# A hybrid decoder trunk on one core: the scan's outputs moved next to the transposes of the next pair of chunks

## The chip, the cores and the metric

The kernel runs on one core of a Trainium2 chip. The metric is the device time of one execution in microseconds (us); several executions are timed and their median is given.

## The reference, cut to what is computed

One sequence of 2048 tokens, width 1024, passes two layers, each `x + RMSNorm_post(mixer(RMSNorm_pre(x)))`. The second mixer is sliding-window attention; the change does not touch it. The first is a Mamba-2 state-space mixer with 32 heads in 8 groups, 16 chunks of 128 tokens:

```python
cb = einsum('bclgn,bcsgn->bcgls', Cc, Bc)                               # scores of a chunk
y_diag = einsum('bcgrls,bcsgrp->bclgrp', cb[:, :, :, None] * decay, x)
states = einsum('bclgn,bcgrl,bclgrp->bcgrpn', Bc, decay_to_end, x)
def step(h, inp):
    s, d = inp
    return h * d[..., None, None] + s, h                                # the scan over chunks
y_off = einsum('bclgn,bcgrpn,bcgrl->bclgrp', Cc, h_in, exp(a_cs))
y = y_diag + y_off
```

Before the scan stand the input projection, a causal convolution of 4 taps and SiLU; after it a gate, a norm and the output projection.

## The kernel before

The first layer takes the tokens in two halves (`hf`) of 1024, and in each the 8 groups one after the other. For a group, `ssm_proj` multiplies the normed input with six blocks of 128 weight columns (B, C, x0, x1, z0, z1), each for two blocks of 512 tokens. All of it is in float32 split into a high and a low part, so a block of 512 tokens is 24 products of 128x512 (three for each of eight row blocks, `mm3`, lines 88 to 92). A block's weights come by a DMA (`wraw`, two buffers), ScalarE makes the high part (`whi`, L150) and GpSimd the low one (`wlo`, L152). The results are evicted by ScalarE (`raw`, `sx`, or the gate `zz`, L733), convolved by VectorE (L749, L753).

`ssm_scan` runs one group behind: while group g is projected, the scan of group g-1 is fed in. It is a generator, and `interleave` calls its next step whenever the projection has advanced by another share of its cost; `SCAN` is the number of steps that the scan of one group has. The steps are:

- `load(c)`: a DMA on SyncE's queue brings `ab` (the cumulative decays of chunk c in 128 partitions). There are four buffers; chunk c+4 takes that of chunk c, which the outputs of chunk c read last.
- `stage1(c)`: on TensorE three transposes and the scores into one PSUM tile `pt` (L779, L780, L783, L784); from it VectorE makes `xd`, `bl`, `xw`, `cbm`, `xl` and ScalarE `bh` (L793) and `xh` (L801). `xl` is the last of this chain (`xw`, then `xh`, then `xl`). From `ab` ScalarE makes the decays: four Relu (L809, the only readers that wait for the load), an Exp on `ab` (L814) and one on `dec` (L816); GpSimd multiplies `ab` (L815), VectorE `dec` (L817).
- `states(c)`: six products `sps` for chunks c and c+1 from `xh`, `xl`, `bh`, `bl`.
- `state(c)`: VectorE adds (`hn`), GpSimd decays (`hd`).
- `outputs(c)`: sixteen small products of 64 output columns, `yt` (L856, L861), for the pair c, c+1; VectorE (L868) and GpSimd (L870) finish `ysb`, and a DMA stores it.

For each pair of chunks four steps come in this order: states and the first state; the second state with stage1 of chunk c+2; stage1 of chunk c+3; outputs of the pair with the loads of c+4 and c+5. Inside `tc.high_priority(offset=60)` stage1's other engines get precedence. The order on each engine is then set by a scheduler, and each engine and the DMA queue keep that order.

The change touches `ssm_scan` (its main loop) and the constant `SCAN`; `run` uses it for each group, and `SCAN - 7` for the rest of the last group's scan, which is fed into the first output pieces (`u`, L251).

Of the kernel before, what the change touches and what calls it, by code (L numbers as in the profile page):

```python
# [35 lines left out]
QW = 1024  # L36
KVW = 256
AIN = 2560
SCAN = 19

# [6 lines left out]
def interleave(main, cost, side, n_side):  # L49

    done, at = 0, 0.0
    for w in main:
        at += w
        want = min(n_side, int(at * n_side / cost))
        while done < want:
            next(side, None)
            done += 1
    drain(side)


class Trunk:
# [694 lines left out]
    def ssm_scan(self, sp, yp, tabs, hf, g, res, yT):  # L756
# [6 lines left out]
        def load(c):  # L763
            if c < 8:
                ab = sp.tile([P, 4, P], F32, tag="ab", name="ab", bufs=4)
                j = c * 8 + g
                nc.sync.dma_start(ab.rearrange("p r l -> p (r l)"), atd[j].partition_broadcast(P))
                abs_.append(ab)

        def stage1(c):  # L770
            if c > 7:
                return
            ab = abs_[c]
            s, o = divmod(c, 4)
            sl = slice(o * P, (o + 1) * P)
            x0, x1, Bt, Ct = (res[n, s] for n in ("x0", "x1", "B", "C"))
            pt = (yp.tile([P, 4, P], F32, tag="y", name="pt", bufs=2) if c % 2
                  else self.tp.tile([P, 4, P], F32, tag="tr", name="pt"))
            nc.tensor.transpose(pt[:, 0, :], x0[:, sl], self.ident)  # L779
            nc.tensor.transpose(pt[:, 1, :], x1[:, sl], self.ident)  # L780
            last = hf == 1 and c == 7
            if not last:
                nc.tensor.transpose(pt[:, 2, :], Bt[:, sl], self.ident)  # L783
            nc.tensor.matmul(pt[:, 3, :], Bt[:, sl], Ct[:, sl], start=True, stop=True)  # L784
            with self.tc.high_priority(offset=60):
                xv = pt[:, 0:2, :].rearrange("p a (h d) -> p (a h) d", d=64)
                xd = sp.tile([P, 4, 64], F32, tag="xd", name="xd", bufs=4)
                hb = dt[:, c, 4 * g:4 * g + 4].unsqueeze(2).to_broadcast([P, 4, 64])
                nc.vector.tensor_tensor(xd, xv, hb, ALU.mult)
                bx = None  # L790
                if not last:
                    bh = sp.tile([P, P], F32R, tag="bh", name="bh")
                    nc.scalar.activation(bh, pt[:, 2, :], AF.Copy)  # L793
                    bl = sp.tile([P, P], F32R, tag="bl", name="bl")
                    nc.vector.tensor_tensor(bl, pt[:, 2, :], bh.bitcast(F32), ALU.subtract)
                    xw = sp.tile([P, 4, 64], F32, tag="xw", name="xw", bufs=1)
                    hb = w2[:, c, 4 * g:4 * g + 4].unsqueeze(2).to_broadcast([P, 4, 64])
                    nc.vector.tensor_tensor(xw, xv, hb, ALU.mult)
                    xf = xw.rearrange("p h d -> p (h d)")
                    xh = sp.tile([P, 256], F32R, tag="xh", name="xh")  # L800
                    nc.scalar.activation(xh, xf, AF.Copy)  # L801
                    xl = sp.tile([P, 256], F32R, tag="xl", name="xl")
                    nc.vector.tensor_tensor(xl, xf, xh.bitcast(F32), ALU.subtract)
                    bx = bh, bl, xh, xl
                cbm = sp.tile([P, P], F32, tag="cbm", name="cbm", bufs=1)
                nc.vector.tensor_tensor(cbm, pt[:, 3, :], self.triu, ALU.mult)
                dec = sp.tile([P, 4, P], F32, tag="dec", name="dec", bufs=4)
                for r in range(4):
                    nc.scalar.activation(dec[:, r, :], ab[:, r, :], AF.Relu, scale=-1.0,  # L809
                                         bias=acs[:, c, 4 * g + r:4 * g + r + 1])  # L810
                ce = None
                if not (hf == 0 and c == 0):
                    ce = ab
                    nc.scalar.activation(ce, ab, AF.Exp)  # L814
                    nc.gpsimd.tensor_tensor(ce, ce, Ct[:, sl].unsqueeze(1).to_broadcast([P, 4, P]), ALU.mult)  # L815
                nc.scalar.activation(dec, dec, AF.Exp, scale=-1.0)  # L816
                nc.vector.tensor_tensor(dec, dec, cbm.unsqueeze(1).to_broadcast([P, 4, P]), ALU.mult)  # L817
            sts.append((xd, bx, dec, ce))

        def states(c):  # L820

            sps = yp.tile([P, 2, 256], F32, tag="st", name="sps")
            for u in range(2):
                if sts[c + u][1]:
                    self.mm3(sps[:, u, :], *sts[c + u][1], True, True)
            return sps

        def decayed(c, h):
            if h is None or c > 7 or (hf == 1 and c == 7):
                return None  # L830
            hd = sp.tile([P, 4, 64], F32, tag="hd", name="hd", bufs=1)
            hb = cd[:, c, 4 * g:4 * g + 4].unsqueeze(2).to_broadcast([P, 4, 64])
            nc.gpsimd.tensor_tensor(hd, h.rearrange("p (h d) -> p h d", d=64), hb, ALU.mult)
            return hd

        def state(c, add, hd):

            if hf == 1 and c == 7:
                return None, None
            hn = self.hsave[g] if (hf == 0 and c == 7) else sp.tile([P, 256], F32, tag="hst", name="hn", bufs=3)  # L840
            if hd is None:
                nc.vector.tensor_copy(hn, add)
            else:
                nc.vector.tensor_tensor(hn, hd.rearrange("p h d -> p (h d)"), add, ALU.add)
            return hn, decayed(c + 1, hn)

        def outputs(c0, hps):

            yt = yp.tile([P, 2, 2 * P], F32, tag="y", name="yt", bufs=2)
            for u in range(2):  # L850
                xd, _, dec, ce = sts[c0 + u]
                for pr in range(2):
                    yo = yt[:, pr, u * P:(u + 1) * P]
                    for e in range(2):
                        r = 2 * pr + e
                        nc.tensor.matmul(yo[64 * e:64 * e + 64], xd[:, r, :], dec[:, r, :],  # L856
                                         start=True, stop=ce is None)
                    if ce is not None:
                        for e in range(2):
                            r = 2 * pr + e  # L860
                            nc.tensor.matmul(yo[64 * e:64 * e + 64], hps[u][:, 64 * r:64 * r + 64], ce[:, r, :],  # L861
                                             start=False, stop=True)
            s, o = divmod(c0, 4)
            sl = slice(o * P, (o + 2) * P)
            ysb = sp.tile([P, 2, 2 * P], F32, tag="ysb", name="ysb")
            for pr in range(2):
                yv = ysb[:, pr, :]
                nc.vector.scalar_tensor_tensor(yv, res[f"x{pr}", s][:, sl], self.dch[:, 2 * g + pr:2 * g + pr + 1],  # L868
                                               yt[:, pr, :], ALU.mult, ALU.add)
                nc.gpsimd.tensor_tensor(yv, yv, res[f"z{pr}", s][:, sl], ALU.mult)  # L870
            t0 = (8 * hf + c0) * P
            nc.sync.dma_start(
                yT[2 * g * P:(2 * g + 2) * P, t0:t0 + 2 * P].rearrange("(a p) t -> p a t", p=P), ysb)
# [1 line left out]
        for c in range(4):  # L875
            load(c)
        stage1(0)
        yield
        stage1(1)
        yield  # L880
        hprev = self.hsave[g] if hf else None
# [2 lines left out]
        for c in range(0, 8, 2):  # L884
            sps = states(c)
            h0 = hprev
            h1, hd = state(c, sps[:, 0, :], hd)
            yield
            hprev, hd = state(c + 1, sps[:, 1, :], hd)
            stage1(c + 2)  # L890
            yield
            stage1(c + 3)
            yield
            outputs(c, (h0, h1))
            load(c + 4)
            load(c + 5)
            yield


# [8 lines left out]
    def run(self, ctx):  # L908
# [19 lines left out]
        with ExitStack() as actx:  # L928
# [35 lines left out]
            for hf in range(2):  # L964
                tabs = {}
                hs, hnext = hnext, []
                for g in range(NG):
# [10 lines left out]
                    cost = 56 if g == 0 else 52 if hf and g == NG - 1 else 58  # L978
                    interleave(self.ssm_proj(ap, hs, hf, g, res, preps, dtg, tail, start), cost, side, SCAN)
                    if dtg:  # L980
# [7 lines left out]
            def head():  # L988
# [5 lines left out]
                yield from pieces[1]  # L994
            interleave(head(), 15, side, SCAN - 7)
        wn = self.bcast(cp, io["pre_norm"][1], tag="wn")
# [62 lines left out]
```

## Time and profile before

| | |
|---|---|
| median of 3 runs | 2584.83 us (2583.25 to 2587.38) |
| the profiled execution | 2584.72 us |
| its span, first to last instruction | 2583.0 us |
| mean granted TensorE clock | 0.995 of full speed |
| the states' products (first and last start) | 117.6 to 1402.2 us of the span |

The page's first part gives each engine's busy time, its fourth the chain of work that ended last. The other views are a timeline of instructions, the instructions of one tile with what they waited for, and busy time by stretches.

### The profile page before, as it was taken

How to read it: one execution, taken by the hardware profiler on the slowest of the kernel's cores; microseconds unless marked ns; L12 is line 12 of the kernel's file. 1: busy time of each engine (PE TensorE's matmuls, PEld its weight loads, DVE VectorE, ACT ScalarE, POOL GpSimd, SP SyncE). 2: the span in 40 equal slices, each digit the busy share in tenths (PEclk: the TensorE clock that was granted, in tenths of full speed). 3: DMA queues.
4: the chain of work that ended last, by engine and by line, in shares of the span. 5: the costliest groups of instructions: out<-in, count | busy, mean ns of one | idle time of the engine just before them, and what ended most of it. 6: DMA issues, size and time to landing. Idle time of an engine off the chain costs nothing.

```text
span 2583.0 us, 38760 instructions
## 1 busy us (share of the span) xinstructions
PE 2527.8 (98%) x14083; PEld 2107.9 (82%) x14083; DVE 1673.7 (65%) x3363; ACT 1274.9 (49%) x3195; POOL 921.6 (36%) x817
## 2 busy tenths in 40 slices
PE   7999999999999999999999999999999999999998
PEld 6878888888777888888887888888888888888787
DVE  6677666766776667666678544447777777767422
ACT  5455555555645555555566422324554455545321
POOL 2344444444434454444445222222222112220222
PEclk9999999999999999999999999999999999999999
DMA  4332223223423222222325332234111121111343
GB/s 127 96 86 64 81 76 87 74 70 78 116 62 105 78 83 77 78 78 78 82 78 174 113 101 90 90 128 140 54 54 58 54 78 54 54 32 58 123 146 120
DMA packets 266656, 224.46 MB, mean 87 GB/s; under 512 B 31136, under 2 KB 229984, under 8 KB 266464
## 3 DMA queue, kind: packets, MB, share of 16 engines
q1 hardware_dynamic: 266464, 221.98, 29.2%
q8 instruction: 111, 1.82, 0.3%
q14 instruction: 81, 0.66, 0.1%
HBM read 179.72 MB, written 42.21 MB: 86 GB/s over the span
## 4 chain that ended last, share of the span: by engine, by line
PE 74%; DVE 10%; POOL 5%; DMA 4%; ACT 4%; issue 4%; SPq 0%; POOLq 0%; ACTq 0%; DVEq 0%
PE u L251 19%; PE ps L90 14%; PE ps L92 14%; PE ps L91 14%; DVE sx L749 2%; DMA ab<-atd 2%; POOL wlo L152 2%; PE sc L420 2%; PE yt L856 2%; PE yt L861 1%; PE ot L474 1%; PE ot L478 1%; DVE dec L817 1%; PE tt L453 1%; POOL ab L815 1%
## 5 line engine op out<-in xcount | busy, mean ns | idle before, releaser
L90 PE MATMUL ps<-hi,whi 128*128 128x512 f32 (+1 forms) x1808 | 725.5, 401 | 9.4 <-ACT whi L150 4.7
L92 PE MATMUL ps<-hi,wlo 128*128 128x512 f32 (+1 forms) x1808 | 706.1, 391 | 4.2 <-POOL wlo L152 4.2
L91 PE MATMUL ps<-lo,whi 128*128 128x512 f32 (+1 forms) x1808 | 704.6, 390 | 0.2 <-DVE lo L140 0.2
L92 PEld LDWEIGHTS ps<-hi,wlo 128*128 128x128 f32 x1808 | 340.7, 188 | 80.2 <-POOL wlo L152 6.1
L90 PEld LDWEIGHTS ps<-hi,whi 128*128 128x128 f32 x1808 | 341.2, 189 | 77.9 <-issue 15.9
L152 POOL TENSOR_TENSOR wlo<-wraw,whi 128x1024 fp32r<-128x1024 f32 x114 | 282.6, 2479 | 319.1 <-ACT whi L150 310.6
L749 DVE SCALAR_TENSOR_TENSOR sx<-raw,cw,sx 128x512 f32<-128x512 f32 x384 | 342.9, 894 | 71.3 <-ACT sx L746 66.5
L91 PEld LDWEIGHTS ps<-lo,whi 128*128 128x128 f32 x1808 | 341.6, 189 | 55.2 <-DVE lo L140 0.8
L251 PE MATMUL u<-ol,yh 128*128 128x512 f32 x768 | 239.6, 393 | 1.0 <-DVE ol L223 0.9
L251 PE MATMUL u<-oh,yh 128*128 128x512 f32 x768 | 240.5, 394 | 0.0
L251 PE MATMUL u<-oh,yl 128*128 128x512 f32 x768 | 237.6, 391 | 0.0
L809 ACT ACTIVATE dec<-ab,acs 128x128 f32<-128x128 f32 x512 | 165.4, 392 | 128.9 <-DMA ab<-atd 114.3
L815 POOL TENSOR_TENSOR ab<-ab,sx 128x512 f32<-128x512 f32 x120 | 168.9, 1409 | 154.5 <-ACT ab L814 140.5
L752 ACT ACTIVATE raw<-sx 128x512 f32<-128x512 f32 x128 | 80.6, 630 | 221.4 <-DVE sx L749 221.3
L90 PE MATMUL ps<-qh,hi 128*128 128x384 f32 x512 | 181.1, 355 | 0.0
L870 POOL TENSOR_TENSOR ysb<-ysb,zz 128x256 f32<-128x256 f32 x128 | 108.1, 861 | 197.9 <-DVE ysb L868 197.7
L235 POOL TENSOR_TENSOR yl<-yr,yh 128x1024 fp32r<-128x1024 f32 (+1 forms) x64 | 119.3, 1864 | 161.3 <-ACT yh L233 161.2
L233 ACT ACTIVATE yh<-yr 128x1024 fp32r<-128x1024 f32 (+1 forms) x64 | 54.1, 845 | 242.3 <-PE u L251 189.3
L91 PE MATMUL ps<-ql,hi 128*128 128x384 f32 x512 | 172.1, 337 | 0.9 <-POOL ql L332 0.9
L251 PEld LDWEIGHTS u<-ol,yh 128*128 128x128 f32 x768 | 143.9, 188 | 34.3 <-DVE ol L223 2.6
L92 PE MATMUL ps<-qh,lo 128*128 128x384 f32 x512 | 171.9, 336 | 0.0
L251 PEld LDWEIGHTS u<-oh,yl 128*128 128x128 f32 x768 | 144.5, 188 | 31.4
(213 smaller groups left out, 4527.7 us busy)
## 6 DMA issues: line engine op xcount, KB each, us to landing
wraw<-in_ssm_w_in SPq DMA_DIRECT2D x98, 512.0 KB, 4.1
ab<-atd SPq DMA_DIRECT2D x128, 256.0 KB, 4.6
xt<-in_x SPq DMA_DIRECT2D x32, 512.0 KB, 4.8
yT<-ysb SPq DMA_DIRECT2D x64, 256.0 KB, 2.5
yr<-yT SPq DMA_DIRECT2D x32, 512.0 KB, 4.0
xt<-x SPq DMA_DIRECT2D x32, 512.0 KB, 4.0
oraw<-in_ssm_w_out SPq DMA_DIRECT2D x16, 512.0 KB, 5.9
x<-xt SPq DMA_DIRECT2D x32, 256.0 KB, 2.1
```

The lines of the kernel that those rows point to most:

```text
L90: nc.tensor.matmul(ps, sh, mh, start=first, stop=False)
L91: nc.tensor.matmul(ps, sh, ml, start=False, stop=False)
L92: nc.tensor.matmul(ps, sl, mh, start=False, stop=last)
L152: nc.gpsimd.tensor_tensor(lo, raw, hi.bitcast(F32), ALU.subtract)
L233: nc.scalar.activation(yh, yr, AF.Copy)
L235: nc.gpsimd.tensor_tensor(yl, yr, yh.bitcast(F32), ALU.subtract)
L251: nc.tensor.matmul(st["u"][h], y[:, k, :], w[:, j, 512 * h:512 * h + 512], start=k0 + k == 0 and m == 0, stop=k0 + k == kt - 1 and m == 2)
L749: nc.vector.scalar_tensor_tensor(sx, raw[:, j:j + BLK], self.cw[:, j, ct:ct + 1], sx, ALU.mult, ALU.add)
L752: nc.scalar.activation(th, sx, AF.Tanh)
L809: nc.scalar.activation(dec[:, r, :], ab[:, r, :], AF.Relu, scale=-1.0, bias=acs[:, c, 4 * g + r:4 * g + r + 1])
L815: nc.gpsimd.tensor_tensor(ce, ce, Ct[:, sl].unsqueeze(1).to_broadcast([P, 4, P]), ALU.mult)
L870: nc.gpsimd.tensor_tensor(yv, yv, res[f"z{pr}", s][:, sl], ALU.mult)
```

## The change

stage1 of chunks 0 and 1 now share one step; in the loop the second state is a step by itself; then one step holds the outputs of the pair, stage1 of the next two chunks and the loads; then a step is empty. The states of the next pair follow. Nothing is computed otherwise.

```diff
--- before.py
+++ after.py
@@ -36,7 +36,7 @@
 QW = 1024
 KVW = 256
 AIN = 2560
-SCAN = 19
+SCAN = 18
 
 
 
@@ -875,7 +875,6 @@
         for c in range(4):
             load(c)
         stage1(0)
-        yield
         stage1(1)
         yield
         hprev = self.hsave[g] if hf else None
@@ -887,13 +886,14 @@
             h1, hd = state(c, sps[:, 0, :], hd)
             yield
             hprev, hd = state(c + 1, sps[:, 1, :], hd)
+            yield
+
+            outputs(c, (h0, h1))
             stage1(c + 2)
-            yield
             stage1(c + 3)
-            yield
-            outputs(c, (h0, h1))
             load(c + 4)
             load(c + 5)
+            yield
             yield
 
 
```

What this makes of the order on the engines is shown at three places for one and the same group, the fourth of the first half. The number behind a tile's name tells its buffers apart.

TensorE, at the outputs of one pair (`yt`), before: the last outputs and what follows them.

```order
L856 MATMUL yt_4141<-dec_4007,xd_3993 64x128 x2
L861 MATMUL yt_4141<-ab_3871,hn_4080 64x128 x2
L856 MATMUL yt_4141<-dec_4007,xd_3993 64x128 x2
L861 MATMUL yt_4141<-ab_3871,hn_4080 64x128 x2
L90 MATMUL ps_4134<-hi_262,whi_4102 128x512
L91 MATMUL ps_4134<-lo_263,whi_4102 128x512
```

And now, at the outputs of chunks 4 and 5:

```order
L856 MATMUL yt_3960<-dec_3824,xd_3810 64x128 x2
L861 MATMUL yt_3960<-ab_3647,hn_3892 64x128 x2
L779 MATMUL pt_3983<-ident_83,sx_3028 128x128
L780 MATMUL pt_3983<-ident_83,sx_3121 128x128
L783 MATMUL pt_3983<-ident_83,sx_2691 128x128
L784 MATMUL pt_3983<-sx_2852,sx_2691 128x128
L779 MATMUL pt_4011<-ident_83,sx_3028 128x128
L780 MATMUL pt_4011<-ident_83,sx_3121 128x128
L783 MATMUL pt_4011<-ident_83,sx_2691 128x128
L784 MATMUL pt_4011<-sx_2852,sx_2691 128x128
L90 MATMUL ps_3953<-hi_108,whi_3949 128x512
```

The outputs were followed by projection products; now the two stage1 of chunks 6 and 7 (`pt_3983`, `pt_4011`) follow them directly. Thirty projection products stand between these and the states' first product.

ScalarE, from `bh` of chunk 6 to the next group's decays, before (`bh_3937`, `xh_3943` are of chunk 6, `bh_3995`, `xh_4001` of chunk 7, `ab_4210`, `ab_4212` the next group's chunks 0 and 1):

```order
L793 ACTIVATE bh_3937<-pt_3930 128x128
L150 ACTIVATE whi_4102<-wraw_4100 128x1024
L742 ACTIVATE raw_3964<-ps_3896 128x512
L801 ACTIVATE xh_3943<-xw_3941 128x256
L744 ACTIVATE halo_345<-ps_3896 128x3
L746 ACTIVATE sx_3968<-ps_3896,cb_333,cw_332 128x512
L793 ACTIVATE bh_3995<-pt_3988 128x128
L801 ACTIVATE xh_4001<-xw_3999 128x256
L733 ACTIVATE zz_4057<-ps_3981 128x512
L752 ACTIVATE raw_3964<-sx_3968 128x512
L809 ACTIVATE dec_4237<-ab_4210,acs_888 128x128 x4
L809 ACTIVATE dec_4287<-ab_4212,acs_888 128x128
```

And now (`xh_3996` is of chunk 6, `xh_4024` of chunk 7):

```order
L793 ACTIVATE bh_3990<-pt_3983 128x128
L793 ACTIVATE bh_4018<-pt_4011 128x128
L809 ACTIVATE dec_4237<-ab_4210,acs_888 128x128 x3
L801 ACTIVATE xh_3996<-xw_3994 128x256
L809 ACTIVATE dec_4237<-ab_4210,acs_888 128x128
L809 ACTIVATE dec_4263<-ab_4212,acs_888 128x128
L816 ACTIVATE dec_4237<-dec_4237 128x512
L809 ACTIVATE dec_4263<-ab_4212,acs_888 128x128 x2
L733 ACTIVATE zz_4057<-ps_3953 128x512
L801 ACTIVATE xh_4024<-xw_4022 128x256
```

Both `xh` stood ahead of every instruction on the next group's `ab`. Now three Relu on `ab_4210` stand ahead of chunk 6's `xh`, and three more, an Exp, two further Relu and a gate `zz` ahead of chunk 7's.

SyncE's queue, the loads of those `ab`, before:

```order
L872 DMA yT_57<-ysb_3863 128x2x256
L148 DMA wraw_4325<-in_ssm_w_in 128x8x128
L767 DMA ab_4210<-atd0_59 128x512
L767 DMA ab_4212<-atd0_59 128x512
L872 DMA yT_57<-ysb_4051 128x2x256
```

And now:

```order
L872 DMA yT_57<-ysb_3771 128x2x256
L148 DMA wraw_4185<-in_ssm_w_in 128x8x128
L148 DMA wraw_4336<-in_ssm_w_in 128x8x128
L767 DMA ab_4210<-atd0_59 128x512
L767 DMA ab_4212<-atd0_59 128x512
L767 DMA ab_4214<-atd0_59 128x512
L872 DMA yT_57<-ysb_3977 128x2x256
```

`ab_4210` stood behind the store of a pair and one weight load, and now behind a store and two. A weight load waits for the `wlo` that last read its buffer.

## Rows read from the trace of the kernel before

**Rows 1.** The page, part 1: busy us, share of the span and instructions of each engine

```profile
PE 2527.8 (98%) x14083; PEld 2107.9 (82%) x14083; DVE 1673.7 (65%) x3363; ACT 1274.9 (49%) x3195; POOL 921.6 (36%) x817
```

**Rows 2.** The page, part 4: who holds the chain that ended last

```profile
PE 74%; DVE 10%; POOL 5%; DMA 4%; ACT 4%; issue 4%; SPq 0%; POOLq 0%; ACTq 0%; DVEq 0%
```

**Rows 3.** Timeline, PE, projection products: start us, us, engine, line, operation, tile

```profile
603.10 0.39 PE L90 MATMUL ps<-hi,whi 128*128 128x512 f32 x1
603.32 0.39 PE L91 MATMUL ps<-lo,whi 128*128 128x512 f32 x1
```

**Rows 4.** Tile sps on PE, 0 to 1360 us: idle before it, until what

```profile
  DVE xl L803: 2.6, 7
  ACT xh L801: 1.8, 3
```

**Rows 5.** The same from 1360 to 1420 us (the scan's last group)

```profile
  DVE xl L803: 2.2, 2
  DVE hn L844: 2.0, 1
```

**Rows 6.** Waits: who waited, for whom, us in total, times, longest

```profile
ACT dec L809 <- DMA ab<-atd: 114.3, 55, 7.9
```

**Rows 7.** Tile ab: its transfers from issue to landing

```profile
DMA to landing us min/median/max: 3.0/4.6/8.6
```

**Rows 8.** Timeline, a load of ab and the ScalarE instruction that waits for it

```profile
646.93 1.01 SPq L767 DMA_DIRECT2D ab<-atd  x2
...
652.03 1.28 ACT L809 ACTIVATE dec<-ab,acs 128x128 f32<-128x128 f32 x4 [3.50 <-DMA ab<-atd]
```

**Rows 9.** Timeline, chunks 6 and 7 of one group: POOL, PE and SP

```profile
579.60 2.38 POOL L152 TENSOR_TENSOR wlo<-wraw,whi 128x1024 fp32r<-128x1024 f32 x1 [0.70 <-ACT whi L150]
...
581.67 0.39 PE L861 MATMUL yt<-ab,hn 128*64 128x128 f32 x4
...
582.01 0.38 SPq L148 DMA_DIRECT2D wraw<-in_ssm_w_in  x1
...
582.45 0.57 SPq L767 DMA_DIRECT2D ab<-atd  x1
```

**Rows 10.** Timeline, ACT, the same group

```profile
584.42 0.42 ACT L801 ACTIVATE xh<-xw 128x256 fp32r<-128x256 f32 x1 [0.92 <-DVE xw L798]
...
587.48 1.56 ACT L809 ACTIVATE dec<-ab,acs 128x128 f32<-128x128 f32 x5
588.95 0.62 ACT L816 ACTIVATE dec<-dec 128x512 f32<-128x512 f32 x1
589.47 0.97 ACT L809 ACTIVATE dec<-ab,acs 128x128 f32<-128x128 f32 x3
...
592.53 0.58 ACT L733 ACTIVATE zz<-ps 128x512 f32<-128x512 f32 x1
```

**Rows 11.** Timeline, DVE, the low half xl of chunk 7

```profile
585.17 0.41 DVE L803 TENSOR_TENSOR xl<-xw,xh 128x256 fp32r<-128x256 f32 x1
```

**Rows 12.** Timeline, PE, the two projection products after outputs

```profile
629.55 0.50 PE L90 MATMUL ps<-hi,whi 128*128 128x512 f32 x1
629.89 0.40 PE L91 MATMUL ps<-lo,whi 128*128 128x512 f32 x1
```

**Rows 13.** Timeline, PE, attention: 64-column products, then transposes of 128 columns

```profile
2037.67 0.60 PE L478 MATMUL ot<-pp,vt 128*64 128x256 f32 x4
2038.21 0.98 PE L136 MATMUL pt<-ident,xt 128*128 128x128 f32 x7
```

**Rows 14.** Timeline, a VectorE instruction beside a GpSimd one

```profile
627.78 2.73 POOL L152 TENSOR_TENSOR wlo<-wraw,whi 128x1024 fp32r<-128x1024 f32 x1 [6.08 <-ACT whi L150]
...
628.19 2.60 DVE L803 TENSOR_TENSOR xl<-xw,xh 128x256 fp32r<-128x256 f32 x1
```

**Rows 15.** Timeline, PE, the projection's wait after the scan of group 0, second half

```profile
818.97 0.50 PE L90 MATMUL ps<-hi,whi 128*128 128x512 f32 x1 [2.66 <-ACT whi L150]
```

**Rows 16.** Windows: length, busy us of PE, PEld, DVE, ACT, POOL, granted clock, DMA share

```profile
821.00:826.00 5.00, 4.55 (x36) 3.57 (x36) 5.00 (x8) 3.21 (x6) 2.78 (x2) 0.66 0.40 105
```

More of the change, by code (lines that the diff above doesn't have):

```diff
@@ L889, in ssm_scan @@
             hprev, hd = state(c + 1, sps[:, 1, :], hd)
-            stage1(c + 2)
-            yield
-            stage1(c + 3)
             yield
             outputs(c, (h0, h1))
+            stage1(c + 2)
+            stage1(c + 3)
             load(c + 4)
             load(c + 5)
+            yield
             yield
```

## The prediction

> **What bounds the kernel now.** I read the page first. TensorE is busy 98% of the span, the next engine 65% [rows 1], and it holds 74% of the chain that ended last [rows 2]. So the kernel is TensorE's stream of products with some holes, and a microsecond in which TensorE stands still is a microsecond of the result. Work on the other engines counts only where TensorE waits for it.
>
> The timeline of TensorE gives the price of the stream: projection products start 0.22 to 0.23 us apart [rows 3]; I use 0.227. Then I looked for the holes that the scan makes, in the tile `sps`, the states' products: up to 1360 us they waited 2.6 us for `xl` and 1.8 us for `xh` [rows 4], in the last group, where few projection products are left as cover, 2.2 us for `xl` and 2.0 us for `hn` [rows 5]. That is all the scan's own chains cost TensorE today, about 9 us, or 0.35%. A change of order can win no more than this and a few turnarounds; it can lose more.
>
> Last, the waits: ScalarE stood 114 us, in 55 waits, for the load of `ab` [rows 6]. Today this costs TensorE nearly nothing, since `xh`, on which the states hang, is ahead of those Relu in ScalarE's order.
>
> **The change part by part.** The number of products, evictions and DMAs stays. What moves is order, and with it the time between a result and its use.
>
> *Turnaround after the outputs.* The outputs use 64 columns of the array. The projection product behind them is followed by the next only 0.34 us later [rows 12] instead of 0.227: 0.11 lost. In attention such products are followed by transposes, as here from now on: seven take 0.98 us [rows 13], the last one's own 0.27 among them: six spacings in 0.71, 0.118 each against 0.109 undisturbed, so some 0.055 is lost. 48 of the 64 outputs have a next pair: 48 x 0.055 = **2.6 us won**.
>
> *The time left for `xl`.* Both stage1 of a pair now stand at one place, and thirty projection products ahead of the states. Counted from the end of the outputs: the transposes and scores are ten passes of about 0.11 (1.0, or 0.9 after the overlap with the outputs' tail), thirty products 6.8, four state products ahead of the one that needs the second chunk's `xl` about 0.12 each. So this `xl` must be there at **8.2 us**. Before, the second stage1 had the same thirty products or these and an output group, but its VectorE and ScalarE work was that of one chunk; now two chunks and the eviction of the outputs share the stretch. For the chunks 0 and 1 nothing waits for a load there, and I count nothing.
>
> *Chunks 6 and 7, first half.* ScalarE now has three Relu on the next group's first `ab` ahead of chunk 6's `xh`, and three more, an Exp, two Relu and a gate ahead of chunk 7's. That `ab` is loaded into the buffer that the outputs directly ahead release, behind a weight load that waits for `wlo`. In the present order `wlo` ended at 581.98, the outputs at 582.06, the weight load was issued at 582.01 and `ab` at 582.45 [rows 9]. I take the same: issue 0.4 after the outputs. The Relu of such a load began 5.1 us after its issue (646.93 to 652.03) [rows 8]; the median to landing is 4.6 [rows 7]. So the first Relu starts at 5.5. Five Relu take 1.5, an Exp leaves ScalarE after 0.52, a gate takes 0.55, `xh` 0.42 [rows 10]: three Relu to 6.4, `xh` to 6.75, two Relu to 7.35, the Exp to 7.9, two Relu to 8.5, the gate to 9.05, `xh` of chunk 7 to 9.45, its `xl` 0.41 [rows 11] to 9.85. Against 8.2 TensorE stands 1.65 us. This happens in the groups 0 to 6 of the first half (for group 7 no table is ready; in the second half chunk 7 makes no state): 7 x 1.65 = **11.6 us lost**. Bounds: if `ab` lands after 3.0 us, the least seen [rows 7], the wait is gone (0); if `wlo` is 0.7 us later, since it now follows a longer burst, 2.35 each, 16.
>
> *Chunks 2 and 3.* ScalarE has an `ab` ahead of the two `xh` here too: chunk 5's, released with the outputs' end in the first half, chunk 4's, released half an output group (0.9) earlier in the second. First half: Relu at 5.15, `xh` of 2 to 5.8, three Relu 6.7, two Exp 7.75, `xh` of 3 to 8.2, `xl` 8.6: 0.4 late. Second half, by the same rows, 8.5: 0.3. Over 15 groups **5 us lost**; bounds 0 and 12. For chunks 4 and 5 the same count ends at 8.2; nothing.
>
> The upper bound there comes from VectorE beside GpSimd: an `xl` of 0.41 took 2.60 us and ended with the `wlo` that had begun just before it [rows 14]. In the new order the multiplication of `ab` on GpSimd falls onto chunk 3's `xl`. I take none of this into the sum, as the bursts may miss each other. The Trainium skill (SBUF — State Buffer, Who interferes with whom) says that a VectorE instruction with two SBUF inputs and a GpSimd instruction that reads SBUF hold a shared port one after the other, the later one blocked to the end of the earlier; the row agrees, and by the rule alone each of these `xl` would end about 0.4 us later, an estimate of 6 us more.
>
> *The last group.* Its outputs, states and transposes stand with few other products between. Chunk 2 and 3's states come 14 short-step products (3.2 us) after the transposes, while four Relu on an `ab` loaded after the outputs stand ahead of `xh`: by the count above 1.7 us for the first chunk and 2 for the second. With the present waits in the two other pairs I take **4 us lost**; bounds -2 and 8.
>
> *What goes away.* The present waits of `sps` before the last group, **4.4 us won** [rows 4]; they sat at chunks whose `xl` now waits for something else.
>
> *The weights after group 0* of each half: the projection waited 2.66 us for `whi` and about as long for `wlo` [rows 15]. `whi` now has one `bh` and `xh` less ahead of it, but `wlo` has two `ysb` multiplications ahead of it on GpSimd. I count 0, between -4 and +3.
>
> Sum: 11.6 + 5 + 4 - 4.4 - 2.6 = +13.6 us. The profiled execution took 2584.72, practically the median of the runs (2584.83); so **2598.5 us**, 0.5% slower.
>
> **The rivals.** A change of 0.2% (5 us) is about what a measurement of this kernel can tell from none.
>
> *No change.* The loads land in time. The wait at chunks 6 and 7 is zero if `ab` is there 3.85 us after the outputs, 3.4 after its issue. For it: the least landing time is 3.0. Against it: the median is 4.6, and 55 waits today [rows 6] show that ScalarE's order reaches for these loads too early. Then +5 at most from chunks 2 and 3 stands against 7 won: 2580 to 2590. The Trainium skill (DMA: Bandwidth & Descriptors, Latency and other measured facts) puts a transfer's fixed cost at about 2 us; an `ab` near that would make this rival true, but the rows of this load say 3.0 to 8.6.
>
> *Faster.* Loads are now asked for four steps ahead of their chunk's stage1 instead of two, so ScalarE is freer at the places where `whi` was late [rows 15], and the pairs' bursts fall where projection covers them. All of the `sps` waits, the turnaround and 4 us at the weights: -11, 2574. It decides whether `xh` of chunk 7 is done before 7.8 us after the outputs.
>
> *Slower still.* The holes at chunks 6 and 7 halve the clock. After the wait of 2.66 us, with another behind it, the granted clock over 5 us was 0.66 of full speed [rows 16], so part of it was at 1.2 GHz; some 1.6 us was lost by that. Seven times 1.6, and GpSimd's blocks of 6 us: +31, 2615.
>
> **How the numbers follow.** The forecast, 2591 to 2610: 0.45. Slower still: 0.15. No change: 0.20. Faster: 0.20. Range 2577 to 2620: it leaves out most of the faster case's end and the far end of the slowest. Faster by over 0.2%: 0.2; within: 0.2; slower: 0.6.
>
> **What would show it.** In the new profile `sps` waits on TensorE for `xh` and `xl` with 15 us or more, at one place per group of the first half, some 9 us after the outputs; ScalarE's wait for `ab` ends just ahead of an `xh`. The product after the transposes starts without the 0.11. Wrong it would be if the holes at `sps` are below 5 us in all, or if `ab` lands within 3.5 us of the outputs.

## The result, and the profile after

The changed kernel takes 2668.72 us (median of 4 runs, 2665.64 to 2671.05) against 2584.34 in runs of the kernel before on the same chip: 1.0326 of it, 95% interval 1.0313 to 1.0338. The prediction was 2598.5 and at most 2620: the sign was right, the loss is six times the one forecast, and it lies above the dearest rival, 2615.

First the page of the changed kernel, part 1, which answers to [rows 1]: busy us, share of the span (2669.1 us, 86.1 more than before) and instructions of each engine.

```profile
PE 2561.5 (96%) x14083; PEld 2131.5 (80%) x14083; DVE 1711.9 (64%) x3363; ACT 1270.9 (48%) x3195; POOL 929.0 (35%) x817
```

TensorE's instructions are 14083 as before, but they are busy 33.7 us longer, and TensorE stands 52.4 us longer (107.6 idle against 55.2). So there are two losses: holes, and products that take longer. The mean granted clock fell from 0.995 to 0.982. Part 4 of the page answers to [rows 2]: TensorE held 74% of the chain and now holds 65%.

```profile
PE 65%; DVE 12%; POOL 7%; ACT 6%; DMA 5%; issue 5%; SPq 0%; POOLq 0%; ACTq 0%; DVEq 0%
```

The tile `sps` on PE, whole span (idle us before it, times), answers to [rows 4, 5], and the view of the waits (us in total, times, longest) to [rows 6]:

```profile
  ACT xh L801: 45.4, 24
  DVE xl L803: 5.8, 5
  DVE hn L844: 1.8, 1
```

```profile
ACT dec L809 <- DMA ab<-atd: 58.7, 39, 5.1
```

The states' products waited 9.2 us in the whole span of the kernel before and wait 53.0 now, nearly all for `xh`: 43.8 of the 52.4. ScalarE waits for `ab` *less* than before (58.7 against 114.3): what counts is not how long it waits but what stands behind. By the starts of the states (how much longer than undisturbed a pair's states take from the product ahead of them to their last one), chunks 6 and 7 of the first half and chunk 6 of the second hold nearly all the holes, one place in a group, as forecast for the first half and not for the second.

By stretches of the timeline (us; each boundary is the first state product of chunks 2 and 3 of the group named, the last one the first product `u`; the rest runs to the end of the span):

| | to group 1 | five groups, to group 6 | to group 1, second half | four groups, to group 5 | to `u` | rest |
|---|---|---|---|---|---|---|
| before | 224.4 | 408.0 | 277.5 | 324.8 | 141.2 | 1207.1 |
| after | 229.9 | 437.8 | 300.5 | 340.6 | 151.3 | 1208.9 |

Below, **M** is the second column, five like groups in which nothing else happens: 29.8 us lost there, 6 per group.

Now one such place, chunks 6 and 7 of group 3, in the timeline of the changed kernel; it answers to [rows 8 to 11]. The lines are sorted by engine. Columns: start us, us, engine, line, operation, tile, in brackets the idle time before it and what ended it.

```profile
430.52 0.39 PE L861 MATMUL yt<-ab,hn 128*64 128x128 f32 x4
430.84 0.33 PE L779 MATMUL pt<-ident,sx 128*128 128x128 f32 x1
431.01 0.27 PE L780 MATMUL pt<-ident,sx 128*128 128x128 f32 x1
...
431.92 0.47 PE L90 MATMUL ps<-hi,whi 128*128 128x512 f32 x1
432.23 0.39 PE L91 MATMUL ps<-lo,whi 128*128 128x512 f32 x1
...
438.62 0.39 PE L92 MATMUL ps<-hi,wlo 128*128 128x512 f32 x1
441.52 0.39 PE L90 MATMUL sps<-xh,bh 128*128 128x256 f32 x1 [2.52 <-ACT xh L801]
...
444.00 0.58 PE L90 MATMUL sps<-xh,bh 128*128 128x256 f32 x1 [1.51 <-ACT xh L801]
...
445.06 0.63 PE L90 MATMUL ps<-hi,whi 128*128 128x512 f32 x1
445.48 0.63 PE L91 MATMUL ps<-lo,whi 128*128 128x512 f32 x1
...
432.06 2.40 POOL L152 TENSOR_TENSOR wlo<-wraw,whi 128x1024 fp32r<-128x1024 f32 x1 [2.24 <-ACT whi L150]
...
434.48 0.37 SPq L148 DMA_DIRECT2D wraw<-in_ssm_w_in  x1
434.95 7.16 SPq L767 DMA_DIRECT2D ab<-atd  x3
...
437.48 0.42 ACT L793 ACTIVATE bh<-pt 128x128 fp32r<-128x128 f32 x2
440.18 0.98 ACT L809 ACTIVATE dec<-ab,acs 128x128 f32<-128x128 f32 x3 [2.28 <-DMA ab<-atd]
441.07 0.40 ACT L801 ACTIVATE xh<-xw 128x256 fp32r<-128x256 f32 x1
...
443.54 0.40 ACT L801 ACTIVATE xh<-xw 128x256 fp32r<-128x256 f32 x1
...
433.22 2.57 DVE L749 SCALAR_TENSOR_TENSOR sx<-raw,cw,sx 128x512 f32<-128x512 f32 x2 [1.34 <-ACT sx L746]
435.71 0.48 DVE L868 SCALAR_TENSOR_TENSOR ysb<-sx,dch,yt 128x256 f32<-128x256 f32 x1
436.10 0.75 DVE L749 SCALAR_TENSOR_TENSOR sx<-raw,cw,sx 128x512 f32<-128x512 f32 x1
436.76 0.75 DVE L789 TENSOR_TENSOR xd<-pt,dt 128x256 f32<-128x256 f32 x2
...
438.42 0.42 DVE L798 TENSOR_TENSOR xw<-pt,w 128x256 f32<-128x256 f32 x1
```

The outputs end at 430.91. The weight load that stands ahead of `ab` on SyncE's queue waits for the `wlo` of 432.06 to 434.46, so `ab` is issued at 434.95, 4.0 us after the outputs. The three Relu begin 5.2 later, at 440.18, chunk 6's `xh` at 441.07: 10.2 us after the outputs. The states were due at 438.85. Chunk 7's `xh` comes 2.5 us later, behind the other Relu, the Exp and the gate. But VectorE is late as well: it had the convolution and an eviction of the outputs ahead and began chunk 6's `xw` only at 438.42. Two of its convolution instructions took 2.57 together, with the `wlo` of 432.06 beside them, where the next took 0.75 alone: about 1.1 us of the lateness. Over the kernel the mean of these instructions rose from 894 to 1025 ns. And after the holes the products start 0.42 apart instead of 0.227: the lower of the two clock levels, 1.2 instead of 2.4 GHz. The window behind them (length, busy us of PE, PEld, DVE, ACT, POOL, granted clock, DMA):

```profile
446.00:452.00 6.00, 6.00 (x19) 4.71 (x18) 0.81 (x2) 1.55 (x2) 1.65 (x3) 0.66 0.00 0
```

### The profile page after: what moved, and what is told of

Its sections match the earlier page's. It is cut to its first block, busy times and chain, and to the rows that moved or that the text cites. A ratio compares the mean times of both kernels' runs of the same rounds, so it can differ in the third digit from the quotient of the medians.

```text
span 2669.1 us, 38619 instructions
## 1 busy us (share of the span) xinstructions
PE 2561.5 (96%) x14083; PEld 2131.5 (80%) x14083; DVE 1711.9 (64%) x3363; ACT 1270.9 (48%) x3195; POOL 929.0 (35%) x817
## 4 chain that ended last, share of the span: by engine, by line
PE 65%; DVE 12%; POOL 7%; ACT 6%; DMA 5%; issue 5%; SPq 0%; POOLq 0%; ACTq 0%; DVEq 0%
PE u L251 19%; PE ps L90 11%; PE ps L91 11%; PE ps L92 11%; DVE sx L749 4%; DMA ab<-atd 4%; POOL wlo L152 3%; PE sc L420 2%; ACT dec L809 1%; PE yt L856 1%; POOL hd L833 1%; PE ot L474 1%; PE yt L861 1%; POOL ab L815 1%; PE ot L478 1%
## 5 line engine op out<-in xcount | busy, mean ns | idle before, releaser
L92 PE MATMUL ps<-hi,wlo 128*128 128x512 f32 (+1 forms) x1808 | 714.9, 395 | 8.6 <-POOL wlo L152 8.6
L91 PE MATMUL ps<-lo,whi 128*128 128x512 f32 (+1 forms) x1808 | 714.5, 395 | 0.2 <-DVE lo L140 0.2
L749 DVE SCALAR_TENSOR_TENSOR sx<-raw,cw,sx 128x512 f32<-128x512 f32 x384 | 393.3, 1025 | 54.6 <-ACT sx L746 48.2
L92 PEld LDWEIGHTS ps<-hi,wlo 128*128 128x128 f32 x1808 | 346.9, 192 | 87.7 <-POOL wlo L152 13.4
L90 PEld LDWEIGHTS ps<-hi,whi 128*128 128x128 f32 x1808 | 348.8, 193 | 74.3 <-issue 8.2
L91 PEld LDWEIGHTS ps<-lo,whi 128*128 128x128 f32 x1808 | 348.0, 192 | 60.2 <-DVE lo L140 0.8
L809 ACT ACTIVATE dec<-ab,acs 128x128 f32<-128x128 f32 x512 | 176.2, 394 | 83.5 <-DMA ab<-atd 58.7
```

The costliest lines, as they stand in the source:

```text
L90: nc.tensor.matmul(ps, sh, mh, start=first, stop=False)
L91: nc.tensor.matmul(ps, sh, ml, start=False, stop=False)
L92: nc.tensor.matmul(ps, sl, mh, start=False, stop=last)
L749: nc.vector.scalar_tensor_tensor(sx, raw[:, j:j + BLK], self.cw[:, j, ct:ct + 1], sx, ALU.mult, ALU.add)
```

## The experiments

Theory A: `xh` of chunks 6 and 7 stands behind Relu that wait for the next group's `ab`. Theory B: the work of two chunks in one stretch is what is late. Theory C, formed after the first four runs: the chain over VectorE from the transposes to `xl` does not fit into 30 products, whatever waits. Beside them, the clock. Ratios are to the kernel before, 95% interval in brackets; `sps` is the idle time before the states.

| run | median us | ratio | `sps` us | clock | M us |
|---|---|---|---|---|---|
| before | | 1 | 9.2 | 0.995 | 408.0 |
| after | 2668.7 | 1.0326 [1.0313, 1.0338] | 53.0 | 0.982 | 437.8 |
| e1 `xh` first everywhere | 2648.6 | 1.0260 [1.0245, 1.0275] | 34.3 | 0.988 | 426.3 |
| e2 six `ab` | 2658.5 | 1.0301 [1.0286, 1.0316] | 55.1 | 0.989 | 427.8 |
| e3 stage1 split | 2675.5 | 1.0362 [1.0347, 1.0378] | 62.9 | 0.985 | 440.2 |
| e4 weights on GpSimd's queue | 2641.1 | 1.0232 [1.0215, 1.0249] | 34.6 | 0.990 | 427.7 |
| e5 three steps | 2610.0 | 1.0110 [1.0095, 1.0125] | 4.9 | 0.993 | 407.5 |
| e6 stage1 first | 2613.3 | 1.0124 [1.0109, 1.0139] | 18.0 | 0.990 | 404.1 |
| e7 e1 and e3 | 2675.9 | 1.0365 [1.0348, 1.0383] | 59.0 | 0.984 | 432.8 |
| e8 filled holes | 2644.5 | 1.0246 [1.0231, 1.0261] | 19.3 | 0.994 | 426.7 |
| e9 stage1 first at 6, 7 | 2603.1 | 1.0081 [1.0066, 1.0097] | 15.0 | 0.992 | 403.4 |
| e10 merge only | 2601.6 | 1.0080 [1.0066, 1.0093] | 19.8 | 0.992 | 405.4 |
| e11 e6 in first half | 2587.5 | 1.0025 [1.0015, 1.0036] | 7.8 | 0.995 | 404.1 |
| e12 e5 in first half | 2591.2 | 1.0034 [1.0022, 1.0047] | 5.0 | 0.994 | 407.5 |
| e13 Relu held for chunks 0, 1 | 2635.5 | 1.0195 [1.0179, 1.0210] | 29.2 | 0.989 | 421.8 |
| e14 merge undone | 2664.0 | 1.0309 [1.0295, 1.0324] | 57.9 | 0.989 | 434.4 |
| e15 e9 and e14 | 2638.6 | 1.0213 [1.0199, 1.0227] | 46.6 | 0.990 | 416.0 |
| e16 best by stage | 2579.9 | 0.9982 [0.9974, 0.9991] | 6.0 | 0.994 | 405.4 |

**e1.** A tiny copy makes each chunk's Relu wait for an earlier `xl`.

```diff
+ self.xls.append(xl)
...
+ k = -2 if hf == 1 and c in (0, 7) else -3
+ held = self.xls[k:k + 1]
+ if held:
+     nc.vector.tensor_copy(dec[0:1, :, 0:1], held[0][0:1, 0:4].bitcast(F32).unsqueeze(2))
  for r in range(4):
...
+ self.xls = []
```

> The changed kernel, with one VectorE copy of four numbers from the xl of two chunks before into dec ahead of the Relu, so that no Relu on a chunk's ab can stand ahead of the xh of the chunk two before. Theory A (xh of chunks 6 and 7 stands behind Relu that wait for the next group's ab): the holes at sps, 53 us in the changed kernel, fall below 15 us, time at half clock from 98 us to below 40 us, 2575 to 2595 us. Theory B (two chunks' stage1 and the eviction in one stretch make VectorE late, whatever ScalarE's order): holes above 30 us remain, now ended by xl, and the time stays above 2640 us.

A miss for theory A: 20 us back, not 75. For theory B the size came (34.3 us, above 2640), but more of the holes end at `xh` (18.5) than at `xl` (14.2). Nor is the test clean: the 126 copies take 41 us of VectorE. At chunk 6 the groups 0 to 6 of the first half have no hole left, but the order of everything moved, and chunks 4 and 5 now lose some 1.1 and 1.3 us in each group, by starts. Timeline there:

```profile
415.15 0.38 PE L91 MATMUL sps<-xl,bh 128*128 128x256 f32 x1 [0.92 <-DVE xl L803]
...
412.53 2.56 DVE L803 TENSOR_TENSOR xl<-xw,xh 128x256 fp32r<-128x256 f32 x1
...
412.28 2.53 POOL L152 TENSOR_TENSOR wlo<-wraw,whi 128x1024 fp32r<-128x1024 f32 x1 [0.88 <-ACT whi L150]
```

An `xl` of 0.41 [rows 11] took 2.56 and ended 0.28 us after the `wlo` beside it, as in [rows 14]. The Trainium skill (SBUF — State Buffer, Who interferes with whom) has this as one port pair held by one of the two; the rows agree, 2.15 us for one instruction.

**e2.** Loads one pair earlier.

```diff
- ab = sp.tile([P, 4, P], F32, tag="ab", name="ab", bufs=4)
+ ab = sp.tile([P, 4, P], F32, tag="ab", name="ab", bufs=6)
...
- self.px = self.pool(ctx, "px", 4)
+ self.px = self.pool(ctx, "px", 3)
```

> The changed kernel with six buffers for ab instead of four (px has three instead of four to make room), so that the load of the next group's first two ab waits for the outputs one pair earlier. The Relu stay ahead of xh. Theory A: the load is there some 20 us earlier, the Relu do not wait, holes at sps below 15 us, 2575 to 2600 us. Theory B: VectorE's work is the same, so holes above 30 us remain and the time stays above 2640 us.

The loads are a pair earlier. At chunk 6 the holes all but go (2.5 us idle in both halves, against 32.2 in the changed kernel), but more come at chunks 3, 5 and 7: 36.9 us for `xl` and 16.4 for `xh` in all. Theory A alone is out.

**e3.** The second stage1 of a pair goes to the empty step.

```diff
  stage1(c + 2)
+ yield
  stage1(c + 3)
  load(c + 4)
  load(c + 5)
  yield
- yield
```

> The changed kernel with the second stage1 of a pair moved into the step that was empty; the outputs are followed by one stage1. Theory A: three Relu on the next group's ab still stand ahead of chunk 6's xh and ab's load is released as before, so the first hole of 1.7 to 3.3 us stays in all 15 groups: 2650 to 2680 us. Theory B: the burst is halved, holes below 20 us, 2580 to 2610 us.

Half the burst, more holes: this speaks against theory B as a burst. It does not settle it, since the second chunk now also has 18 products instead of 30 from its transposes to its states; e6, where the burst is whole, does.

**e4.** The weights on another queue.

```diff
- nc.sync.dma_start(raw, src.rearrange("(k p) c -> p k c", p=P))
+ nc.gpsimd.dma_start(raw, src.rearrange("(k p) c -> p k c", p=P))
```

> The changed kernel with the weight loads of the projection issued from GpSimd's queue, so that SyncE's queue holds the loads of ab and no weight load that waits for wlo ahead of them. Theory A with the weight load as the cause of the lateness: the next group's first ab is issued within 0.6 us of the outputs' end instead of 4.4 us, chunk 6's xh is in time and chunk 7's at most 2 us late, holes at sps below 20 us, 2585 to 2615 us, if the weights themselves do not come later. Theory A without it (the load is late for another reason) or theory B: above 2640 us.

Timeline of the same place in e4 (outputs end at 429.0):

```profile
428.21 9.47 SPq L767 DMA_DIRECT2D ab<-atd  x3
...
436.36 1.27 ACT L809 ACTIVATE dec<-ab,acs 128x128 f32<-128x128 f32 x4
437.53 0.41 ACT L801 ACTIVATE xh<-xw 128x256 fp32r<-128x256 f32 x1
...
436.69 0.41 DVE L798 TENSOR_TENSOR xw<-pt,w 128x256 f32<-128x256 f32 x1
...
439.46 0.41 DVE L798 TENSOR_TENSOR xw<-pt,w 128x256 f32<-128x256 f32 x1
...
439.90 0.42 ACT L801 ACTIVATE xh<-xw 128x256 fp32r<-128x256 f32 x1
...
437.99 0.38 PE L90 MATMUL sps<-xh,bh 128*128 128x256 f32 x1 [0.89 <-ACT xh L801]
...
440.37 0.38 PE L90 MATMUL sps<-xh,bh 128*128 128x256 f32 x1 [1.42 <-ACT xh L801]
```

The load is issued at 428.21, before the outputs end, and no Relu waits for it. So the weight load was why `ab` was late in the changed kernel. Still `xh` is late, 0.89 and then 1.42 us at chunk 7: the first cannot start before `xw` ends at 437.10, after the states were due (436.95), and then waits 0.43 for Relu that no longer wait but still take their turn; the second starts as its `xw` ends, at 439.9. The Trainium skill (Trainium Kernel Development and Optimization, Key Constraints) says that issuing DMAs from several engines saves only a sequencer's issue time. Here it also took a load out from behind another's wait, and the kernel with this edit is 28 us faster.

**e5.** Both states in one step, three steps behind the transposes.

```diff
  h1, hd = state(c, sps[:, 0, :], hd)
- yield
  hprev, hd = state(c + 1, sps[:, 1, :], hd)
  yield
  outputs(c, (h0, h1))
...
+ yield
  yield
  yield
```

> The changed kernel with both states of a pair in one step and the step so gained added behind: the outputs with the transposes come one step earlier, 48 products instead of 30 stand between the transposes and the states. Theory C (what decides is the time from the transposes to the states: the chain over VectorE needs 7 to 10 us, and 30 products leave it 7): holes at sps below 12 us in all, half clock below 40 us, 2575 to 2600 us. Rival D (the time is only moved: the outputs, now one step after the states, wait for dec, ab or hn): holes at yt above 20 us, above 2620 us.

As theory C had it: 48 products instead of 30, and the holes at `sps` fall to 4.9 us with the outputs still directly ahead of the transposes. But 18 more products, 4.1 us, are time for the waiting Relu as well, so e5 does not tell theory C from A; e13 does. Rival D takes part of it back: the outputs wait for `hn` (tile `yt` on PE):

```profile
  DVE hn L844: 19.5, 31
  DVE dec L817: 7.7, 3
```

**e6.** Both stage1 ahead of the outputs in the same step.

```diff
- outputs(c, (h0, h1))
  stage1(c + 2)
  stage1(c + 3)
+ outputs(c, (h0, h1))
```

> The changed kernel with the outputs behind the two stage1 in the same step instead of ahead of them. The transposes are 1.8 us earlier against the states, the xh stand ahead of the Relu on the next ab, the next ab is released as late as before. Theory C with theory A: both causes are weakened, holes at sps below 25 us, 2590 to 2625 us. If only the burst of two chunks counts (theory B): the work of two chunks is still in one stretch, holes above 40 us, above 2640 us.

In M the whole loss is gone, with the work of two chunks still in one stretch: theory B as a burst is out. The largest rest lies in the second half, some 13 us at chunk 6, by starts.

**e7.** The diffs of e1 and e3 together.

> Both edits at once: Relu held behind the xl of two chunks before, and the second stage1 of a pair in the step that was empty. Theory A and B together (Relu on ab ahead of xh, and two chunks in one stretch on VectorE): holes at sps below 15 us, 2575 to 2605 us. Theory C: the second chunk has only 18 products (4.1 us) from its transposes to its states, so its xl is late in most pairs: holes above 30 us, above 2640 us.

As theory C had it: the second chunk with 18 products is late (holes at chunks 3, 5 and 7).

**e8.** Useless products in the holes. ScalarE and GpSimd keep their order exactly, VectorE but for a few instructions.

```diff
  if sts[c + u][1]:
+     if c == 6:
+         for _ in range(8 - 2 * u):
+             nc.tensor.matmul(sps[:, u, 0:P], self.ident, self.triu, start=True, stop=True)
...
```

> The changed kernel with eight useless products of 128 columns ahead of the states of chunk 6 and six ahead of those of chunk 7, some 0.9 to 1.8 us of work on TensorE at each of the places where it stands; the order on all other engines is the same. If part of the loss is the clock that is halved after these holes (98 us at half clock now): below 60 us at half clock, and in spite of 350 more instructions the time falls to 2635 to 2655 us. If the clock does not answer to filled holes: 2665 to 2690 us.

Timeline of e8 at the same place, and the PE line of its page:

```profile
433.04 1.95 PE L827 MATMUL sps<-triu,ident 128*128 128x128 f32 x16
435.44 0.39 PE L90 MATMUL sps<-xh,bh 128*128 128x256 f32 x1 [0.46 <-ACT xh L801]
...
438.07 0.39 PE L90 MATMUL sps<-xh,bh 128*128 128x256 f32 x1 [0.33 <-ACT xh L801]
...
438.87 0.40 PE L90 MATMUL ps<-hi,whi 128*128 128x512 f32 x1
439.11 0.40 PE L91 MATMUL ps<-lo,whi 128*128 128x512 f32 x1
```

```profile
PE 2574.4 (97%) x14435; PEld 2154.6 (81%) x14435; DVE 1709.9 (65%) x3363; ACT 1269.8 (48%) x3195; POOL 929.0 (35%) x817
```

TensorE does 352 instructions more, some 43 us of work (1.95 for 16), and the kernel is 24 us faster. The old instructions are busy some 30 us less, and the products behind the holes start 0.24 apart again: the clock was a loss of its own, some 30 of the 33.7 us by which busy time had grown.

**e9.** e6 at one pair alone.

```diff
+ if c == 4:
+     stage1(c + 2)
+     stage1(c + 3)
  outputs(c, (h0, h1))
- stage1(c + 2)
- stage1(c + 3)
+ if c != 4:
+     stage1(c + 2)
+     stage1(c + 3)
```

> The changed kernel with the two stage1 ahead of the outputs at chunks 6 and 7 alone; the other pairs keep outputs and then transposes. If the loss of the middle groups sits at chunks 6 and 7 alone, the five middle groups of the first half take 405 to 412 us from states to states (before 408.0, changed kernel 437.8, with every pair turned round 404.1), and the whole 2610 to 2630 us. If the other pairs share it, above 420 us and 2640 us.

With the 18 steps of the change the place is settled: this pair alone gives 66 us back, 34.4 of it in M, more than the whole loss there.

**e10.** The kernel before, with this part of the change alone.

```diff
- SCAN = 19
+ SCAN = 18
...
  stage1(0)
- yield
  stage1(1)
```

> The kernel before with the first part of the change alone: stage1 of chunks 0 and 1 in one step and 18 steps, the loop as it was. If the loss comes from the loop: within 10 us of the kernel before. If merging the first two stage1 costs a part: 2600 us or more, with new holes at the states of chunks 0 and 1.

A miss for the theory that all comes from the loop: the merge with its 18 steps costs 20 us by itself, none in M, 8.0 in the four groups of the second half (holes at chunks 1 and 5, up to 1.6 each) and 8.3 in the last.

**e11, e12.** The loops of e6 and e5 in the first half only, in the kernel before.

```diff
- interleave(self.ssm_proj(ap, hs, hf, g, res, preps, dtg, tail, start), cost, side, SCAN)
+ interleave(self.ssm_proj(ap, hs, hf, g, res, preps, dtg, tail, start), cost, side, SCAN if hf and g else 18)
...
  stage1(0)
- yield
+ if hf:
+     yield
  stage1(1)
...
+ if hf == 0:
+     yield
+     hprev, hd = state(c + 1, sps[:, 1, :], hd)
+     yield
+     stage1(c + 2)
+     stage1(c + 3)
+     outputs(c, (h0, h1))
+     load(c + 4)
+     load(c + 5)
+     yield
+     yield
+     continue
```

That is e11; in e12 the branch holds the lines of e5's loop in the same way.

> First half with the loop of e6 (both stage1 of a pair and then its outputs), second half with the loop of the kernel before. By stages: e6 took 3.9 us less than before in the middle of the first half and 2.5 less ahead of it, 11 more around the change of halves. If the stages keep their own times: 2570 to 2590 us, no more than 0.3% from before. If the order in one half disturbs the other: above 2590 us.

> First half with the loop of e5 (outputs, transposes, then three steps to the states), second half with the loop of the kernel before. By stages: e5 took 3 us more ahead of the middle, 0.5 less in it, 12 less around the change of halves and lost its time in the second half. If the stages keep their own times: 2568 to 2580 us, faster than before by 0.1 to 0.6%. If not: above 2585 us.

The stages keep their times, but neither beats the kernel before. The "12 less" of e5 in the text of e12, and the 266 us that rest on it in that of e16, are a miscount of the states; counted rightly e5 takes 5.2 us *more* around the change of halves.

**e13.** e1 for the next group's first two chunks alone.

```diff
- if held:
+ if held and c < 2:
```

> The changed kernel with the Relu held back behind an earlier xl only for chunks 0 and 1 of each group, so that the xh of chunks 6 and 7 stand ahead of all Relu on the next group's ab; chunks 2 to 5 keep their order. If the waiting Relu are the whole cause at chunks 6 and 7: the five middle groups of the first half take 405 to 412 us (changed kernel 437.8), the whole 2600 to 2620 us. If VectorE's chain has too little time in 30 products whatever ScalarE's order: 415 to 430 us, the waits at sps now end at xl as well, the whole 2625 to 2655 us.

Timeline of the same place (outputs end at 422.5, states due at 430.5):

```profile
428.37 0.75 DVE L789 TENSOR_TENSOR xd<-pt,dt 128x256 f32<-128x256 f32 x2
...
430.03 0.42 DVE L798 TENSOR_TENSOR xw<-pt,w 128x256 f32<-128x256 f32 x1
...
431.87 0.42 DVE L798 TENSOR_TENSOR xw<-pt,w 128x256 f32<-128x256 f32 x1
...
430.48 0.42 ACT L801 ACTIVATE xh<-xw 128x256 fp32r<-128x256 f32 x1 [0.96 <-DVE xw L798]
432.32 0.42 ACT L801 ACTIVATE xh<-xw 128x256 fp32r<-128x256 f32 x1 [1.43 <-DVE xw L798]
...
430.95 0.39 PE L90 MATMUL sps<-xh,bh 128*128 128x256 f32 x1 [0.33 <-ACT xh L801]
...
432.79 0.38 PE L90 MATMUL sps<-xh,bh 128*128 128x256 f32 x1 [0.88 <-ACT xh L801]
```

No Relu stands ahead of `xh` now, ScalarE waits for `xw`, and the states still come 0.5 and 1.0 us late. This is theory C, and its forecast came, but for one sign: the holes still end at `xh` (20.5 of 29.2 us), not at `xl`. The 30 copies take 3.3 us of VectorE. M gives back 16.0 of 29.8: so a little over half of the loss there goes with the Relu ahead of `xh`, and the rest, by the lines, with VectorE's chain, each with the clock that its holes cost.

**e14, e15.** First two stage1 apart again, alone (e14) and with the diff of e9 (e15).

```diff
- SCAN = 18
+ SCAN = 19
...
  stage1(0)
+ yield
  stage1(1)
```

> The changed kernel with the first two stage1 in two steps again and 19 steps: the loop of the change alone. If merge and loop add up: 2669 less 20, 2640 to 2655 us. If the loop alone costs the whole: 2660 to 2680 us.

> The changed kernel with the first two stage1 in two steps and both stage1 of chunks 6 and 7 ahead of the outputs; at chunks 2 to 5 the outputs are still followed at once by the transposes. If the two causes are the whole loss: 2580 to 2592 us. If the order costs something at the other pairs: above 2598 us.

In both the second forecast came: the loop alone costs nearly the whole (e14), and the order costs something at the other pairs (e15). The causes do not add up. With 19 steps the holes move, in the second half to chunk 5 (some 30 us by starts in e15), and in the first half chunks 3 and 5 wait with the old order at those pairs. Which wait is last there was not followed.

**e16.** Each stage with its best order.

```diff
- interleave(self.ssm_proj(ap, hs, hf, g, res, preps, dtg, tail, start), cost, side, SCAN)
+ interleave(self.ssm_proj(ap, hs, hf, g, res, preps, dtg, tail, start), cost, side, 18 if (hf == 0 and g <= 6) else SCAN)
...
+ if hf == 0 and g < 6:
...
+ if hf == 0:
...
```

The first branch holds e6's loop, the second e5's; the first two stage1 share a step in groups 0 to 5 of the first half.

> Groups 0 to 5 of the first half with the loop of e6, groups 6 and 7 with the loop of e5, second half as in the kernel before. If the stages keep their own times: 222, 404 and 266 us for the first three stages, 2555 to 2568 us, faster than before by 0.5 to 1%. If the change from one loop to the other disturbs the order: 2570 to 2590 us.

It beats both kernels, the one before by 0.18% [0.09 to 0.26], a small gain: its runs reach from 2575.7 to 2584.0 us, those before from 2581.1 to 2587.0. The first two stages took 221.5 and 405.4 as expected, the third 278.2 and not 266, by the miscount; so the time lies in the second range, but not for its reason.

## Why the prediction was wrong

**What bounds the kernel, and the place: right.** Holes for `xh` at one place per group, with the Relu on `ab` directly ahead of it, were named as the sign, and are there. e9 shows that this pair carries most of the loss.

**Chunks 6 and 7, first half (11.6 us): mis-sized.** By starts the seven groups lose some 36 us there, without the slower products behind the states. The first step that failed is "I take the same: issue 0.4 after the outputs". Measured: 4.0. In the kernel before, `wlo` ended with the outputs [rows 9]; the outputs moved against the projection and `wlo` did not, so `wlo` came 3.6 us after them. The bound of 0.7 for it was a guess from no row. The sum had chunk 6's `xh` begin 6.4 and end 6.75 after the outputs; it began at 10.2. e4 shows that the weight load is why `ab` is late.

**The time left for `xl` (8.2 us): the count was right, the chain was not.** The states were due 7.9 us after the outputs. But I counted ScalarE's row alone and let `xw` be there when it was wanted. VectorE takes its instructions in order, with the convolution and the outputs' eviction ahead: `xw` began 7.5 us after the outputs in the changed kernel and in e13. This is what e13 left, and e5, e6 and e9 gave the chain more time. In the traces of e13 and e4 chunk 7's `xw` also starts only after chunk 6's `xl`; the kernel has one buffer for `xw`, so the second hole may hang on the first. Two buffers for `xw` were not tried.

**Second half, chunk 6: left out.** "In the second half chunk 7 makes no state" is true, but chunk 6 was late too: some 16 us by starts in its first six groups.

**Chunks 2 and 3 (5 us): nothing there.** In the middle groups no hole at all. **Last group (4 us)**: 10.1 in the last stretch, which takes in the two groups before it as well. **Chunks 0 and 1 (nothing):** wrong as an argument: the merge alone costs 20 us (e10), though undoing it in the changed kernel gives back only 5 (e14). **Weights after group 0 (0):** right, the waits for `whi` and `wlo` there are 8.6 us in all, before and now. New are short waits for `wlo` at six other places of the second half, 3.4 us. **Turnaround (2.6 won):** right as far as it went. The first two transposes start 0.17 apart (430.84, 431.01), some 0.06 more than the usual 0.11. But the second product behind transposes comes after 0.31 (431.92, 432.23) instead of 0.227; this was so before the change too, at 120 places, and is now at 61, some 5 us won that the sum does not have. So the sign that the product behind the transposes would start without the loss did not come.

**The clock: left out of the sum.** The rival "slower still" had the mechanism, 1.6 us for each of seven holes; it got 0.15 and 11 us. It was 33.7 us of busy time, some 30 of which e8 got back. Holes of this size should have carried that price in the sum itself: [rows 16] showed it for one.

## What to carry to other kernels

When a step is moved, count each engine in its order between the moved step and its first reader, with the work that is already there, not the one engine whose waits the profile shows today. A transfer's issue time follows the slowest wait ahead of it on its queue, and that wait may be tied to another stream: look at what keeps its place when the step moves. Where TensorE is the bound, price a hole with the half clock that followed it here, 2.4 us in the place shown. Giving the chain 48 products instead of 30 (59 us, e5), or the transposes ahead of the outputs at the one tight pair (66, e9), was worth more than any edit against a single wait (10 to 33 us, e1, e2, e4, e13).

## What the runs showed that I had not expected

- Holes of 2.5 and 1.5 us close together cost 12 products at 0.427 instead of 0.227 us, 2.4 us more, in the place shown; 352 useless instructions made the kernel 24 us faster (e8).
- Edits against one wait moved holes to other chunks (e1, e2), and two edits that give 66 and 5 us back alone (e9, e14) give 30 together (e15).
- A weight load issued by GpSimd landed in 4.7 us (median) instead of 4.0, and GpSimd was busy 105 us longer for the 114 that moved there, 98 of this layer's projection and 16 of the attention's (e4).
